# Splitting W_out's plain blocks in the projection's narrow groups instead of at the end of attention

## The chip, the cores and the metric

The kernel runs on one core of a Trainium2 chip. The metric is device time in microseconds of one execution, as the median over runs. A profile is of one execution, taken by the hardware profiler; its own time is given beside its span. The engines are PE (TensorE, matrix products), DVE (VectorE), ACT (ScalarE), POOL (GpSimd) and SP (SyncE, which here only issues DMAs).

## The reference

One decoder layer of width 1024 over 2048 tokens, in float32, followed by a last norm:

```python
n = rmsnorm(x)
# one projection W_in gives: GLA q, k, v, output gate and low-rank forget gate; attention q, k, v
a = gla_mixer(...)        # gated linear attention, 4 heads (dk 64, dv 128), chunks of 64
b = dilated_attention(...)  # 8 heads of 64; windows/dilations (128,1), (512,4), (2048,16), with a bias by distance
h = x + concat(a, b) @ W_out          # W_out is 1024 x 1024
h = h + relu(rmsnorm(h) @ W1) ** 2 @ W2   # 1024 -> 4096 -> 1024
y = rmsnorm_final(h)
```

The GLA half of the mix is normalised per head, and its gain `gn` is folded into the first 512 rows of W_out.

## The kernel before, in words

**Products in three passes.** A float32 factor is split into a part `hi`, rounded by ACT, and the rest `lo` = value − `hi`, by DVE. `mm3` (L139) issues hi·hi, lo·hi and hi·lo as three matmuls. So every matrix that PE uses is first split by ACT and DVE. The large products go through schemes with seven products for eight blocks, for which sums and differences of blocks are split.

**The projection** (up to about 490 us) runs over two halves of the tokens, in nine groups of columns of W_in for each half (NG = 9). Groups 2 to 7 are "narrow", 128 columns wide in each half of the columns, with seven products ("jobs") each, in the order 1, 2, 6, 5, 7, 3, 4. A job is twelve matmuls of 128x512. `prep` (L291) runs two jobs ahead of PE: ACT makes `hi` (L304), DVE makes `lo` (L306 or L308) and the sums of blocks of the weights, in place (L310, L313, L314, L316), into a ring of three buffers. SP loads the rows of W_in for the narrow groups, POOL those of the last, wide group (both L284, tile `wraw`); `finish` takes the results (L383, L384) and issues their stores (`qD`, `kD` and others). In the second half the narrow groups run from about 354 to 470 us, some 19 us each, and the last group, `gv`, from 470 to 490.

**Attention** (about 490 to 855 us) is written as 160 units, with GLA's steps, the loads of the next heads and the combination of the three branches (`mx`, L1439; its loads `combine_load`) issued between them at numbered units (`at_unit`, L1257; `plan`). PE's transposes there are L950, its products with v L969; ACT copies the probabilities (`pt`, L957) and evaluates the exponentials (L941), DVE makes the masked scores (L940) and some of the copies.

**W_out's product** follows (about 853 to 1032 us). Its matrix is taken as four column and row blocks. Some blocks are used as sums, made during attention by `sum_wo` and read by `mix_wo`; four, numbered 1, 12, 2 and 3, are used as they are ("plain"): by `product0` (L1605) for products 1, 2 and 3, and by `plain_rows` (L1619) for four tiles that take no scheme. `load_wo` (L1183) loads one of the eight 128-row pieces c of W_out (512 KB, tile `woraw`, L1188) at each of the units NU−28, NU−25, ..., and splits it at once: for c < 4 in two halves into the blocks 1 and 12 (ACT L1193 with the gain `gn`, DVE L1194), for c ≥ 4 in one piece into `wo` (ACT L543, DVE L544). That is between 788 and 847 us.

**Order and memory.** A scheduler with a cost model orders the instructions of each engine, unless `keep_in_program_order` holds one in its place; an engine then carries out its instructions strictly in that order, and waits for others by semaphores. All large tiles come from one pool of 25 slots of 128x2112 float32 (`slot`, L127); a slot's new tenant waits until the last reader of the old one is done. SP, ACT and POOL can issue DMAs, each in its own queue.

Of the kernel before, what the change touches and what calls it, by code (L numbers as in the profile page):

```python
# [10 lines left out]
F32 = mybir.dt.float32  # L11
FR = mybir.dt.float32r
I32 = mybir.dt.int32
AF = mybir.ActivationFunctionType
OP = mybir.AluOpType
# [3 lines left out]
D = 1024  # L19
NT = S // 128  # L20
HT = NT // 2
CH = D // 128
# [7 lines left out]
AHEAD, LAG = 3, 2  # L30
# [84 lines left out]
def emit(tc, a, stop=99):  # L115
    nc = tc.nc
    V, A, G, T, SP = nc.vector, nc.scalar, nc.gpsimd, nc.tensor, nc.sync
# [9 lines left out]
    def slot(name, dt=F32, n=SLOT):  # L127

        return up.tile([128, SLOT], dt, name=name, tag="u", bufs=25)[:, :n]

    def view(t, shape):
        n = int(np.prod(shape))
        names = "abcd"[:len(shape)]
        return t[:, :n].rearrange(f"p ({' '.join(names)}) -> p {' '.join(names)}", **dict(zip(names, shape)))
# [4 lines left out]
    def mm3(out, sh, sl, mh, ml, first, last, **kw):  # L139
        T.matmul(out, sh, mh, start=first, stop=False, **kw)  # L140
        T.matmul(out, sl, mh, start=False, stop=False, **kw)  # L141
        T.matmul(out, sh, ml, start=False, stop=last, **kw)  # L142
# [19 lines left out]
    gn = stats[:, 44:]  # L162
# [357 lines left out]
    def bias_rows():  # L520

        rb, oh, rbo = xp[:33, :8], view(xp[:33, 8:], (3, 384)), view(bp[:8], (3, 384))
        SP.dma_start(rb[:32], a["rel_bias"])
        SP.dma_start(oh, a["c_onehot"])
        V.memset(rb[32:33], NEG)
        yield
        V.tensor_scalar(rb[:32], rb[:32], -1.0, None, op0=OP.mult)
        for d in range(3):
            p = ps("d")
            T.matmul(p[:8, :384], rb, oh[:, d], start=True, stop=True)  # L530
            V.tensor_copy(rbo[:, d], p[:8, :384])
        SP.dma_start(rowD, rbo)
        yield
# [8 lines left out]
    def split(hi, lo, src):  # L542
        A.activation(hi, src, AF.Copy)  # L543
        V.tensor_tensor(lo, src, hi.bitcast(F32), op=OP.subtract)  # L544
# [60 lines left out]
    def second_half():  # L605

        b = [view(bp[:, 512 * q:], (4, 128)) for q in range(4)]
        for i in range(4):
            for k in range(2):
                x_load(8 + 4 * k + i, xp[:, D * k:D * k + D])  # L610
            yield
            for k in range(2):
                xt = xp[:, D * k:D * k + D]
                ss = stat()
                tc.keep_in_program_order(A.activation(bp[:, :D], xt, AF.Square, accum_out=ss))
                r = rstd_of(ss, D)
                V.scalar_tensor_tensor(xt, xt, r, gB, op0=OP.mult, op1=OP.mult)
            yield
            for k in range(2):
                for q, pv in enumerate(transposed(xp[:, D * k:], pin=True, by=perm)):  # L620
                    A.activation(b[2 * k + q], pv, AF.Copy)
                yield
            (b11, b21, b12, b22), (t2, t4, t3) = b, [view(xp[:, 512 * q:], (4, 128)) for q in range(3)]
            V.tensor_tensor(b12, b12, b11, op=OP.subtract)
            V.tensor_tensor(t2, b22, b12, op=OP.subtract)
            for j, v in ((2, b21), (1, b11), (5, b12), (6, t2), (3, b22), (4, t4), (7, t3)):
                if j == 5:
                    yield
                    V.tensor_tensor(t4, b21, t2, op=OP.subtract)
                    V.tensor_tensor(t3, t2, b11, op=OP.subtract)  # L630
                SP.dma_start(nTD[j - 1][:, :, i * 128:i * 128 + 128], v)
            yield
# [165 lines left out]
    SP.dma_start(w2b[33:50].bitcast(F32), w2raw[33:].bitcast(F32))  # L798
    for gT in gTs:
        A.activation(gT, ident, AF.Copy, scale=0.0)  # L800
    other, back, bias = second_half(), [], bias_rows()
    for at in range(7, len(jobs)):
        g = jobs[at][0]
        prep(at + 2)
        if at in (7 * NG - 7, 7 * NG - 6):
            back.extend(reload(2 * (at - 7 * NG + 7) + k) for k in range(2))
        for i in range(4 if groups[g % NG][2] > 128 else 1):
            ready = gated[:]
            product(at, i)()
            for t in ready:  # L810
                gate_product(t)
                gated.remove(t)
        if behind and chained(g):
            f, *args = behind.pop(0)
            f(*args)
        if back and at >= 7 * NG - 5:
            back.pop(0)()
            back.pop(0)()
        if at in OTHER:
            next(other)  # L820
        if at == len(jobs) - 14:
            heads = load_head(0)
        if at in (len(jobs) - 13, len(jobs) - 10, len(jobs) - 9):
            next(heads)
        if at in (7 * NG + 3, 7 * NG + 5):
            next(bias)
        if 7 * NG + 8 <= at < 7 * NG + 44 and at % 3 == 0:
            spread_bias(2 - (at - 7 * NG - 8) // 12, (at - 7 * NG - 8) // 3 % 4 * 2)
# [336 lines left out]
                    A.activation(st[:, j], st[:, j], AF.Copy, scale=w[:, j:j + 1])  # L1165
                yield

    wo = a["w_out"].rearrange("o (c p) n -> p (o c) n", p=128)
    WO, WB, loaded = {}, {}, []

    def block_view(j, c):

        if (j, c // 2) not in WB:
            WB[j, c // 2] = view(slot(f"wb{j}", FR), (2, 2, 512))
        return [WB[j, c // 2][:, c % 2, i] for i in range(2)]

    def wo_part(j, c):

        if j in (2, 3):
            return [WO[c][:, i, 512 * (j - 2):512 * (j - 2) + 512] for i in range(2)]  # L1180
        return block_view(j, c)

    def load_wo(n):  # L1183
        for _ in range(n):
            c = (4, 0, 1, 5, 2, 3, 6, 7)[len(loaded)]
            loaded.append(c)
            raw = slot("woraw")[:, :D]
            SP.dma_start(raw, wo[:, c])  # L1188
            if c < 4:
                for j, n in ((1, 0), (12, 1)):  # L1190
                    hi, lo = block_view(j, c)
                    r = raw[:, 512 * n:512 * n + 512]
                    A.activation(hi, r, AF.Copy, scale=gn[:, c:c + 1])  # L1193
                    V.scalar_tensor_tensor(lo, r, gn[:, c:c + 1], hi.bitcast(F32), op0=OP.mult, op1=OP.subtract)  # L1194
            else:
                w = WO[c - 4] = view(slot("wo", FR), (2, D))
                split(w[:, 0], w[:, 1], raw)

    wtD = dram.tile([4, 128, 2 * D], F32, name="wtD")

# [56 lines left out]
    def at_unit(n, *f):  # L1257
        plan.setdefault(n, []).append(f)
# [45 lines left out]
    NU = len(units)  # L1304
# [1 line left out]
    for n, x in enumerate(sums_wo):  # L1306
        at_unit(8 + AHEAD + n, next, x)
    for i in range(8):
        at_unit(NU - 28 + 3 * i + AHEAD, load_wo, 1)
    gla = gla_steps()  # L1310
    for k in range(-AHEAD, NU + LAG):
        tr, pv, sc = iter(()), iter(()), iter(())
# [292 lines left out]
    def product0(g):  # L1605
        p, j = g // 7, order[g % 7]
        if j in (1, 2, 5):
            held0[j] = ps({1: "a", 2: "o", 5: "d"}[j])
        b = held0[{6: 1, 7: 1, 4: 1, 3: 5}.get(j, j)]
        c = combs0[g % 6]  # L1610
        for k in range(4):
            mm3(b, c[:, 0, k], c[:, 1, k], *wo_part(j, k), k == 0 and j in (1, 2, 5), k == 3, skip_group_check=True)
        e, n = {1: (0, 0), 2: (0, 0), 6: (0, 1), 3: (0, 1), 5: (1, 1), 7: (1, 1), 4: (1, 0)}[j]
        x = xhs[p][:, e, 512 * n:512 * n + 512]
        V.tensor_tensor(x, b, x, op=OP.add)
        if j in (3, 4):
            row_done(p, j == 4)
# [9 lines left out]
    for at in range(4):  # L1627
        p, e = divmod(at, 2)
        m = nxt
        if at == 0:  # L1630
            load_x(0, True)
            tc.keep_in_program_order(SP.dma_start(gM, bcast_row(a["mlp_norm_g"], D)))
        if at in (0, 2):
            nxt = plain_rows(p, 1)
            load_mix(p + 1)
            load_x(p + 1)
        if at == 1:
            nxt = plain_rows(1, 0)
        mix_wo(at)
        if at == 3:  # L1640
            for n in range(4):
                raw_block(2, n % 2, n // 2)
            load_mix(3)
            for g in range(14, 16):
                prep0(g)
        b = [ps("ad"[e]), ps("ad"[e])]
        parts_ = 2 if at < 2 else 1
        for q in range(parts_):
            for n in range(2):
                for c in range(q * CH // parts_, (q + 1) * CH // parts_):  # L1650
                    mm3(b[n], m[:, 0, c], m[:, 1, c], *wo_part(((1, 12), (2, 3))[c // 4][n], c % 4), c == 0, c == CH - 1)
                if q == parts_ - 1:
                    x = xhs[p][:, e, 512 * n:512 * n + 512]
                    V.tensor_tensor(x, b[n], x, op=OP.add)
        next_norm()
        row_done(p, e)
        if at == 3:
            prep0(16)
# [270 lines left out]
```

## Time and profile before

| | |
|---|---|
| time, median of 3 runs | 2239.28 us (2235.93 to 2239.9) |
| profiled execution | 2235.3 us, span 2233.5 us, clock 0.998 |
| busy: PE, DVE, ACT, POOL | 99%, 74%, 55%, 24% of the span |
| narrow groups of the second half | about 354 to 470 us |
| attention | about 490 to 855 us |
| splits of W_out's plain blocks | 792.1 (first on ACT) to 845.5 us (last on DVE starts) |

A row of a timeline gives start and duration in us, the engine, the line of the kernel, the tile written and those read, the shape, and in brackets how long the engine stood idle before it and what ended that. A row of a window gives for each engine the busy time and, behind the x, the number of instructions, then the granted clock as a share of full speed, the busy share of the 16 DMA engines and what they moved in GB/s. A landing is the time from a DMA's issue to its arrival.

### The profile page before, as it was taken

The numbers are of one execution on the slowest core, as the hardware profiler recorded it, in microseconds if no ns is written. First come the engines' busy times: TensorE is split into PE (matmuls) and PEld (weight loads), VectorE is DVE, ScalarE is ACT, GpSimd is POOL, SyncE is SP. The second block draws the span as 40 slices with busy tenths as digits, with TensorE's granted clock in tenths as the row PEclk, the third lists the DMA queues.
The fourth block names the chain that finished last, engine by engine and source line by source line (L and its number), as shares of the span: only waits on it lengthen the run. The fifth ranks groups of instructions, "written<-read, shape, count | busy, mean of one in ns | idle before, by whom it ended". The sixth has DMA issues, their size and how long they took to land.

```text
span 2233.5 us, 34965 instructions
## 1 busy us (share of the span) xinstructions
PE 2208.3 (99%) x12420; PEld 1918.8 (86%) x12420; DVE 1650.9 (74%) x3093; ACT 1236.2 (55%) x2420; POOL 528.4 (24%) x527
## 2 busy tenths in 40 slices
PE   9999999999999999999999999999999999999998
PEld 8988998899999988887788887888888888888877
DVE  8676766657777788778776788777686697576798
ACT  7365524437888885546555566555555433333446
POOL 1000000026586673000000000000007222042462
PEclk9999999999999999999999999999999999999999
DMA  6566855677967966768644456555489998677775
GB/s 208 176 216 190 268 152 170 208 216 260 322 226 238 278 199 245 239 227 269 208 147 142 140 178 192 158 174 161 130 287 284 307 295 270 216 247 253 253 258 197
DMA packets 331763, 491.50 MB, mean 220 GB/s; under 512 B 20615, under 2 KB 225050, under 8 KB 320836
## 3 DMA queue, kind: packets, MB, share of 16 engines
q1 hardware_dynamic: 307282, 381.97, 52.7%
q0 software_dynamic: 16960, 54.60, 9.7%
q10 hardware_dynamic: 7346, 52.70, 6.2%
q8 instruction: 98, 1.61, 0.3%
q14 instruction: 77, 0.63, 0.1%
HBM read 335.25 MB, written 158.66 MB: 221 GB/s over the span
## 4 chain that ended last, share of the span: by engine, by line
PE 75%; issue 16%; DMA 3%; DVE 3%; POOL 2%; ACT 1%; POOLq 0%; ACTq 0%; SPq 0%; DVEq 0%
PE ps_a L141 8%; PE ps_a L142 8%; PE ps_a L140 8%; PE ps_c L141 6%; PE ps_c L142 6%; PE ps_c L140 6%; PE ps_a L969 4%; PE ps_d L141 4%; PE ps_d L142 4%; PE ps_d L140 4%; PE ps_o L140 3%; PE ps_o L141 3%; PE ps_o L142 3%; PE ps_d L950 3%; PE ps_c L932 2%
## 5 line engine op out<-in xcount | busy, mean ns | idle before, releaser
L543 ACT ACTIVATE cb<-bs 128x1024 fp32r<-128x1024 f32 x104 | 110.1, 1060 | 286.4 <-PE ps_c L141 95.4
L544 DVE TENSOR_TENSOR cb<-bs,cb 128x1024 fp32r<-128x1024 f32 x104 | 161.5, 1553 | 136.8 <-ACT cb L543 136.4
L1749 POOL TENSOR_TENSOR bs<-bs,rb 128x1024 f32<-128x1024 f32 x60 | 173.9, 2904 | 312.8 <-DMA bs<-w_ff 280.8
L544 DVE TENSOR_TENSOR w1comb<-w1raw,w1comb 128x512 fp32r<-128x512 f32 x224 | 153.5, 687 | 92.5 <-ACT w1comb L543 92.4
L1456 POOL DMA_DIRECT2D w1raw<-w_ff x64 | 48.1, 752 | 701.4 <-DVE w1comb L544 524.9
L543 ACT ACTIVATE w1comb<-w1raw 128x512 fp32r<-128x512 f32 x224 | 139.8, 627 | 89.1 <-PE ps_c L142 26.1
L969 PE MATMUL ps_a<-v,pt 128*128 128x65 f32 x1200 | 178.6, 253 | 1.8 <-ACT pt L957 1.8
L969 PEld LDWEIGHTS ps_a<-v,pt 128*128 128x128 f32 x1200 | 173.9, 195 | 3.8 <-ACT pt L957 2.7
L941 ACT ACTIVATE pe<-pe,O 128x256 f32<-128x256 f32 (+1 forms) x384 | 154.9, 453 | 13.5 <-DVE O L940 12.3
L950 PE MATMUL ps_d<-ident,pe 128*128 128x128 f32 x600 | 159.5, 280 | 1.2 <-ACT pt L957 1.1
L304 ACT ACTIVATE wcomb<-wraw 128x512 fp32r<-128x512 f32 (+2 forms) x119 | 90.4, 759 | 114.4 <-PE ps_a L141 54.6
L940 DVE CUSTOM_DVE_ANT_0 pe<-ps_c,nb 128x256 f32<-128x256 f32 (+1 forms) x384 | 125.7, 360 | 34.3 <-PE ps_d L950 23.0
L140 PE MATMUL ps_c<-hb,w1comb 128*128 128x512 f32 x320 | 124.6, 390 | 0.8 <-DVE acc L1545 0.8
L141 PE MATMUL ps_c<-hb,w1comb 128*128 128x512 f32 x320 | 124.5, 389 | 0.0
L142 PE MATMUL ps_c<-hb,w1comb 128*128 128x512 f32 x320 | 124.0, 389 | 0.0
L141 PE MATMUL ps_c<-cb,ca 128*128 128x512 f32 x312 | 121.4, 389 | 0.0
L142 PE MATMUL ps_c<-cb,ca 128*128 128x512 f32 x312 | 121.4, 389 | 0.0
L140 PE MATMUL ps_c<-cb,ca 128*128 128x512 f32 x312 | 121.4, 389 | 0.0
L544 DVE TENSOR_TENSOR ca<-ra,ca 128x1024 fp32r<-128x1024 f32 x84 | 119.7, 1426 | 0.1
L306 DVE TENSOR_TENSOR wcomb<-wraw,wcomb 128x512 fp32r<-128x512 f32 (+2 forms) x77 | 73.2, 950 | 53.3 <-ACT wcomb L304 53.2
L950 PEld LDWEIGHTS ps_d<-ident,pe 128*128 128x128 f32 x600 | 108.6, 186 | 1.7 <-ACT pt L957 1.3
L1530 ACT ACTIVATE acc<-acc 128x512 f32<-128x512 f32 x96 | 60.6, 632 | 68.3 <-DVE acc L1549 31.7
(490 smaller groups left out, 7174.4 us busy)
## 6 DMA issues: line engine op xcount, KB each, us to landing
ra<-actD ACTq DMA_DIRECT2D x50, 1024.0 KB, 7.4
actD<-ring SPq DMA_DIRECT2D x176, 256.0 KB, 3.0
rb<-w_ff SPq DMA_DIRECT2D x88, 512.0 KB, 5.9
bs<-w_ff SPq DMA_DIRECT2D x72, 512.0 KB, 6.6
w1raw<-w_ff POOLq DMA_DIRECT2D x64, 512.0 KB, 5.5
k<-kD SPq DMA_DIRECT2D x16, 1024.0 KB, 9.0
rb<-hTD SPq DMA_DIRECT2D x28, 512.0 KB, 5.0
wraw<-w_in SPq DMA_DIRECT2D x48, 256.0 KB, 3.7
```

The source lines that it names most:

```text
L140: T.matmul(out, sh, mh, start=first, stop=False, **kw)
L141: T.matmul(out, sl, mh, start=False, stop=False, **kw)
L142: T.matmul(out, sh, ml, start=False, stop=last, **kw)
L304: A.activation(hi, src, AF.Copy, scale=sc)
L306: V.tensor_tensor(lo, src, hi.bitcast(F32), op=OP.subtract)
L543: A.activation(hi, src, AF.Copy)
L544: V.tensor_tensor(lo, src, hi.bitcast(F32), op=OP.subtract)
L940: V.tensor_tensor_reduce(p, s, bias, scale=1.0, scalar=BIG, op0=OP.add, op1=OP.min, accum_out=nm)
L941: A.activation(p, p, AF.Exp, bias=nm, scale=-1.0)
L950: T.transpose(pb[:, i * 128:i * 128 + 128], src, ident)
L969: T.matmul(self.b.opsum[:, n % 4], self.pt[:, i * 128:i * 128 + 128], self.b.v[:, blk, cols], start=first, stop=last)
L1749: (engines or ((G,), (V, V))[len(sums) - 1])[e].tensor_tensor(v, v, r, op=OP.add if op == "+" else OP.subtract)
```

## The change

The eight 128-row pieces of W_out are loaded and split in the second half's narrow groups. A generator, `split_wo`, has two slots: one for two raw pieces of 512 KB (`wsum`), one for two split pieces (`wsplit`, each a half row of 512 columns as `hi` and `lo`). POOL loads the raw pieces; sixteen splits by ACT (L815 of the new file, held in program order) and DVE (L816) follow, two after each job 6 and two after each job 5 of groups 3 to 6 of the half; POOL stores each split piece (512 KB, L817) to DRAM, and after every second one loads the next raw piece (L819). At the end of attention, at the units at which `load_wo` ran, `load_parts` loads 1 MB of split pieces by SP (L1207) into the slots from which PE reads; neither ACT nor DVE takes part.

```diff
+    wsD = {j: dram.tile([2, 128, 2, 2, 512], F32, name=f"wsD{j}") for j in (1, 12, 2, 3)}
+    def split_wo():
+        raw, pieces = view(slot("wsum"), (2, D)), view(slot("wsplit", FR), (2, 2, 512))
+        for c in range(2):
+            G.dma_start(raw[:, c], wo[:, c])
+        yield
+        for n in range(16):
+            c, h = divmod(n, 2)
+            p = pieces[:, h]
+            r = raw[:, c % 2, 512 * h:512 * h + 512]
+            w = gn[:, c:c + 1] if c < 4 else 1.0
+            tc.keep_in_program_order(A.activation(p[:, 0], r, AF.Copy, scale=w))
+            V.scalar_tensor_tensor(p[:, 1], r, w, p[:, 0].bitcast(F32), op0=OP.mult, op1=OP.subtract)
+            G.dma_start(wsD[((1, 12), (2, 3))[c // 4][h]][c % 4 // 2, :, c % 2], p.bitcast(F32))
+            if h and c < 6:
+                G.dma_start(raw[:, c % 2], wo[:, c + 2])
+            yield
...
+        if at == 7 * NG + 18:
+            next(of_wo)
+        if NG + 3 <= g < NG + 7 and jobs[at][1] in (6, 5):
+            for _ in range(2):
+                next(of_wo)
...
-    def load_wo(n):
...
+    def load_parts(j, h):
+        t = slot(f"wb{j}", FR, 2048)
+        WB[j, h] = view(t, (2, 2, 512))
+        SP.dma_start(t.bitcast(F32), wsD[j][h].rearrange("p c i n -> p (c i n)"))
...
-        at_unit(NU - 28 + 3 * i + AHEAD, load_wo, 1)
+        at_unit(NU - 28 + 3 * i + AHEAD, load_parts, *((1, 0), (12, 0), (1, 1), (12, 1), (2, 0), (3, 0), (2, 1), (3, 1))[i])
...
-            mm3(b, c[:, 0, k], c[:, 1, k], *wo_part(j, k), k == 0 and j in (1, 2, 5), k == 3, skip_group_check=True)
+            mm3(b, c[:, 0, k], c[:, 1, k], *block_view(j, k), k == 0 and j in (1, 2, 5), k == 3, skip_group_check=True)
```

The order of ACT in a narrow group of the second half, before. `acc` are the results of the projection, `wcomb` the split weights of a job, `ps_a` and `ps_c` the accumulators:

```order
328 L304 ACTIVATE wcomb<-wraw 128x4x128 x2
329 L383 ACTIVATE acc<-acc 128x512
330 L482 ACTIVATE acc<-ps_a 128x4x16x8
331 L304 ACTIVATE wcomb<-wraw 128x4x128
332 L484 ACTIVATE acc<-ps_c 128x4x16x8
333 L304 ACTIVATE wcomb<-wraw 128x4x128 x2
334 L383 ACTIVATE acc<-acc 128x512
335 L304 ACTIVATE wcomb<-wraw 128x4x128
336 L383 ACTIVATE acc<-acc 128x512
```

The same place of ACT in the changed kernel:

```order
331 L304 ACTIVATE wcomb<-wraw 128x4x128 x2
332 L383 ACTIVATE acc<-acc 128x512
333 L482 ACTIVATE acc<-ps_a 128x4x16x8
334 L815 ACTIVATE wsplit<-wsum,stats 128x512 x2
335 L304 ACTIVATE wcomb<-wraw 128x4x128
336 L484 ACTIVATE acc<-ps_c 128x4x16x8
337 L304 ACTIVATE wcomb<-wraw 128x4x128 x2
338 L383 ACTIVATE acc<-acc 128x512
339 L304 ACTIVATE wcomb<-wraw 128x4x128
340 L815 ACTIVATE wsplit<-wsum,stats 128x512
341 L383 ACTIVATE acc<-acc 128x512
342 L815 ACTIVATE wsplit<-wsum,stats 128x512
```

Four splits of W_out now stand among a group's seven splits of W_in, two ahead of four L304 and two behind them.

The order of DVE around one change of groups, before. The L310 here reads the next group's rows of W_in:

```order
434 L306 TENSOR_TENSOR wcomb<-wraw,wcomb 128x4x128
435 L310 TENSOR_TENSOR wraw<-wraw 128x512
436 L384 TENSOR_TENSOR acc<-acc 128x512
437 L313 TENSOR_TENSOR wraw<-wraw 128x512
438 L492 TENSOR_TENSOR acc<-ps_c,acc 128x4x16x8
439 L306 TENSOR_TENSOR wcomb<-wraw,wcomb 128x4x128
440 L314 TENSOR_TENSOR wraw<-wraw 128x512
441 L384 TENSOR_TENSOR acc<-acc 128x512
```

And in the changed kernel:

```order
438 L306 TENSOR_TENSOR wcomb<-wraw,wcomb 128x4x128
439 L384 TENSOR_TENSOR acc<-acc 128x512
440 L313 TENSOR_TENSOR wraw<-wraw 128x512
441 L492 TENSOR_TENSOR acc<-ps_c,acc 128x4x16x8
442 L306 TENSOR_TENSOR wcomb<-wraw,wcomb 128x4x128
443 L816 SCALAR_TENSOR_TENSOR wsplit<-wsum,stats,wsplit 128x512
444 L314 TENSOR_TENSOR wraw<-wraw 128x512
445 L384 TENSOR_TENSOR acc<-acc 128x512
446 L310 TENSOR_TENSOR wraw<-wraw 128x512
447 L816 SCALAR_TENSOR_TENSOR wsplit<-wsum,stats,wsplit 128x512
```

L310 has moved from directly behind an L306 to behind seven more instructions, one of them a split of W_out; at the other changes of groups it moves by three to eight.

More of the change, by code (lines that the diff above doesn't have):

```diff
@@ L800, in emit @@
         A.activation(gT, ident, AF.Copy, scale=0.0)
+    wo = a["w_out"].rearrange("o (c p) n -> p (o c) n", p=128)
+    wsD = {j: dram.tile([2, 128, 2, 2, 512], F32, name=f"wsD{j}") for j in (1, 12, 2, 3)}
[15 more added lines that the diff above has]
+            yield
+    of_wo = split_wo()
     other, back, bias = second_half(), [], bias_rows()
@@ L1166, in gla_steps @@
                 yield
-    wo = a["w_out"].rearrange("o (c p) n -> p (o c) n", p=128)
-    WO, WB, loaded = {}, {}, []
+    WB = {}
     def block_view(j, c):
@@ L1175, in block_view @@
         return [WB[j, c // 2][:, c % 2, i] for i in range(2)]
[L1177 to L1181, printed above, removed]
-    def load_wo(n):
[L1184 to L1197, printed above, removed]
+    def load_parts(j, h):
+        t = slot(f"wb{j}", FR, 2048)
+        WB[j, h] = view(t, (2, 2, 512))
+        SP.dma_start(t.bitcast(F32), wsD[j][h].rearrange("p c i n -> p (c i n)"))
     wtD = dram.tile([4, 128, 2 * D], F32, name="wtD")
@@ L1650, in emit @@
                 for c in range(q * CH // parts_, (q + 1) * CH // parts_):
-                    mm3(b[n], m[:, 0, c], m[:, 1, c], *wo_part(((1, 12), (2, 3))[c // 4][n], c % 4), c == 0, c == CH - 1)
+                    mm3(b[n], m[:, 0, c], m[:, 1, c], *block_view(((1, 12), (2, 3))[c // 4][n], c % 4), c == 0, c == CH - 1)
                 if q == parts_ - 1:
```

## The prediction

> **What bounds the kernel now.** I read the page first (busy time, then the chain), then windows of 5 us over the end of attention, then PE's own timeline there with what ended each gap, then ACT's and DVE's timelines at those gaps, and last the narrow groups into which the work moves.
>
> ```profile
> PE 2208.3 (99%) x12420; PEld 1918.8 (86%) x12420; DVE 1650.9 (74%) x3093; ACT 1236.2 (55%) x2420; POOL 528.4 (24%) x527
> PE 75%; issue 16%; DMA 3%; DVE 3%; POOL 2%; ACT 1%; POOLq 0%; ACTq 0%; SPq 0%; DVEq 0%
> ```
>
> PE is busy for 99% of the span and carries three quarters of the chain. The change leaves PE's matmuls alone, so it can only give or take where PE stands still or runs slowly. The stage that loses its splitting work is such a place. Columns: PE busy (matmuls), PEld, DVE, ACT, POOL, granted clock, DMA share, GB/s.
>
> ```profile
> 800.00:805.00 5.00, 5.00 (x46) 4.82 (x46) 5.00 (x21) 4.43 (x13) 4.85 (x7) 1.00 0.34 132
> 805.00:810.00 5.00, 5.00 (x48) 4.60 (x47) 2.90 (x7) 3.52 (x13) 4.51 (x11) 1.00 0.90 266
> 810.00:815.00 5.00, 3.03 (x18) 2.09 (x17) 4.01 (x17) 2.93 (x6) 2.53 (x6) 0.90 0.93 316
> 815.00:820.00 5.00, 3.74 (x17) 3.74 (x18) 4.96 (x12) 3.39 (x10) 5.00 (x4) 0.50 0.62 215
> 820.00:825.00 5.00, 4.23 (x37) 4.03 (x35) 3.95 (x12) 4.28 (x10) 5.00 (x5) 0.91 0.28 104
> 825.00:830.00 5.00, 4.72 (x43) 4.72 (x44) 4.57 (x16) 5.00 (x14) 4.47 (x6) 1.00 0.74 225
> 830.00:835.00 5.00, 5.00 (x52) 5.00 (x51) 4.01 (x13) 4.80 (x15) 0.00 (x0) 1.00 1.07 314
> 835.00:840.00 5.00, 5.00 (x47) 4.89 (x46) 4.98 (x17) 4.71 (x17) 2.41 (x8) 1.00 0.99 295
> 840.00:845.00 5.00, 3.93 (x34) 3.54 (x33) 4.57 (x11) 4.40 (x9) 3.97 (x8) 1.00 0.73 232
> 845.00:850.00 5.00, 4.66 (x46) 4.68 (x47) 5.00 (x11) 4.94 (x14) 4.46 (x3) 1.00 1.00 329
> ```
>
> Undisturbed, PE does (46+48+52+47)/4 = 48.25 matmuls in 5 us. From 810 to 825 it does 18+17+37 = 72 where 144.75 were due: 72.75 missing, 7.5 us. From 825 to 830 and from 840 to 850 another 5.25+16.5 are missing, 2.3 us. So 9.8 us is lost here. PE's timeline names the gaps (start, duration, and in brackets the idle time before and what ended it):
>
> ```profile
> 812.43 1.13 PE L1160 MATMUL ps_o<-gla 128*128 128x256 f32 x4 [1.48 <-DVE gla L1107]
> 816.26 1.97 PE L969 MATMUL ps_a<-v,pt 128*128 128x65 f32 x8 [1.62 <-ACT pt L957]
> 825.28 0.66 PE L950 MATMUL ps_d<-ident,pe 128*128 128x128 f32 x4 [1.05 <-ACT pt L957]
> 845.34 0.53 PE L1439 MATMUL ps_c<-ident,mx 128*128 128x128 f32 x3 [1.41 <-DVE O L940]
> ```
>
> What stood ahead of the first, the second and the fourth:
>
> ```profile
> 810.23 1.34 ACT L1193 ACTIVATE wb<-woraw,stats 128x512 fp32r<-128x512 f32 x2 [1.71 <-DMA woraw<-w_out]
> 813.50 1.06 ACT L543 ACTIVATE wo<-woraw 128x1024 fp32r<-128x1024 f32 x1 [1.84 <-DMA woraw<-w_out]
> 842.04 2.00 DVE L544 TENSOR_TENSOR wo<-woraw,wo 128x1024 fp32r<-128x1024 f32 x1 [0.39 <-ACT wo L543]
> ```
>
> The first gap: ACT holds still 1.71 us for a raw row of W_out, DVE's L1194 waits for ACT's result, and the L1107 that PE needs is queued behind it. The second: ACT holds still 1.84 us for the next row, then splits it (1.06), and the `pt` copy L957 comes after. The fourth: 2.00 us of L544 stand on DVE ahead of the L940 that PE waits for. All four gaps together are 1.48+1.62+1.05+1.41 = 5.6 us; the other 4.2 of the 9.8 come mostly from the clock granted in 815–820, 0.50.
>
> **The change, part by part.** *Removed at the end of attention.*
>
> ```profile
> L1193 ACT ACTIVATE wb<-woraw,stats x8: 707/713/726, 801.3 to 830.5; 128x512 fp32r<-128x512 f32 x8
> L1194 DVE SCALAR_TENSOR_TENSOR wb<-woraw,stats,wb x8: 661/752/1743, 802.6 to 831.3; 128x512 fp32r<-128x512 f32 x8
> L543 ACT ACTIVATE wo<-woraw x4: 1043/1058/1058, 792.1 to 842.7; 128x1024 fp32r<-128x1024 f32 x4
> L544 DVE TENSOR_TENSOR wo<-woraw,wo x4: 1226/1656/2001, 793.2 to 845.5; 128x1024 fp32r<-128x1024 f32 x4
> DMA to landing us min/median/max: 3.6/3.8/4.1
> ```
>
> ACT loses 8×0.713 + 4×1.058 = 9.9 us, DVE 8×0.752 + 4×1.656 = 12.6 us, both from a stretch in which each is over 80% busy. More than the work, the waits go: nothing on ACT or DVE waits for `woraw` any more. All that is late next there is other attention work, which kept PE supplied in 800–810 and 830–840. The most that can come back is 9.8 us; the least is the idle of the two gaps whose ACT waited for a row, 1.48+1.62 = 3.1. I take the 7.5 us of 810–825 and leave the 2.3 us of the two later gaps to what follows.
>
> The Trainium skill ("TensorE: Matmul & The Clock Gate", Part 1: The HAM clock gate) has the clock halve only after an idle window of about 3.4 us. Here it stands at 0.50 after gaps of 1.48 and 1.62 us with work between them, so no single gap reaches the rule's length. By the rule alone the low clock would have another cause and stay, and the gain would be the idle only; the trace decides, since the low clock follows the two gaps and occurs in none of the other nine windows below 0.90.
>
> *Added at the end:* the eight loads are of 1 MB instead of 512 KB, 4.2 MB more on SP's queue, ahead of the `mx` and `gla` loads that attention itself waits for. The DMA shares of the ten windows leave 0.66+0.10+0.07+0.38+0.72+0.26+0.27 = 2.46 windows, 12.3 us, free; 4.2 MB at the 329 GB/s of the last row are 12.7. So they just fit, and a transfer behind one comes later.
>
> ```profile
> ra<-actD ACTq DMA_DIRECT2D x50, 1024.0 KB, 7.4
> ```
>
> The nearest row of that size lands in 7.4 us, 3.6 more than the 3.8 of a `woraw` row. The new loads themselves are issued by 838 and needed after 853, so their own 7.4 us lies hidden. For others behind them I take the 2.3 us already left out, between 0 and 3.6.
>
> *Added in the narrow groups:* sixteen ACT splits at the 0.713 of L1193, 11.4 us, sixteen on DVE at 0.752, 12.0 us, and 24 DMAs of 512 KB on POOL's queue, 12.6 MB. What stands there now, in windows of 10 us:
>
> ```profile
> 380.00:390.00 10.00, 10.00 (x47) 8.19 (x46) 5.58 (x11) 6.43 (x16) 0.00 (x0) 1.00 1.01 247
> 390.00:400.00 10.00, 10.00 (x46) 8.28 (x45) 8.02 (x13) 4.81 (x8) 0.00 (x0) 1.00 0.54 189
> 400.00:410.00 10.00, 10.00 (x46) 8.29 (x45) 4.60 (x7) 4.87 (x7) 0.00 (x0) 1.00 1.05 279
> 410.00:420.00 10.00, 9.73 (x43) 7.51 (x42) 7.43 (x11) 3.98 (x7) 0.00 (x0) 1.00 0.32 109
> 420.00:430.00 10.00, 10.00 (x46) 8.27 (x45) 4.81 (x8) 4.51 (x9) 0.00 (x0) 1.00 0.98 306
> 430.00:440.00 10.00, 10.00 (x46) 8.29 (x45) 8.27 (x13) 3.96 (x7) 0.00 (x0) 1.00 0.77 227
> 440.00:450.00 10.00, 10.00 (x46) 8.29 (x45) 4.50 (x7) 3.50 (x6) 1.51 (x2) 1.00 0.51 151
> 450.00:460.00 10.00, 10.00 (x46) 8.29 (x45) 4.44 (x7) 3.01 (x6) 0.00 (x0) 1.00 0.30 94
> sum 80.00, PE 79.73 PEld 65.41 DVE 47.65 ACT 35.07 POOL 1.51; mean PE 9.97 PEld 8.18 DVE 5.96 ACT 4.38 POOL 0.19
> ```
>
> In 80 us ACT has 45 us free and DVE 32, so 11.4 and 12.0 fit beside PE. Two waits are the danger. DVE's timeline shows the first, the transfers' rows the sizes (the last line is the landing of the 512 KB stores of `qD` in 355–470):
>
> ```profile
> 391.44 0.69 DVE L310 TENSOR_TENSOR wraw<-wraw 128x512 f32<-128x512 f32 x1 [1.88 <-DMA wraw<-w_in]
> 412.50 0.69 DVE L310 TENSOR_TENSOR wraw<-wraw 128x512 f32<-128x512 f32 x1 [3.46 <-DMA wraw<-w_in]
> 430.56 0.69 DVE L310 TENSOR_TENSOR wraw<-wraw 128x512 f32<-128x512 f32 x1 [2.03 <-DMA wraw<-w_in]
> wraw<-w_in SPq DMA_DIRECT2D x16, 256.0 KB, 5.6
> DMA to landing us min/median/max: 3.0/3.3/7.2
> ```
>
> First, DVE already stands 1.9 to 3.5 us at L310 in each of three groups, for the next group's rows of W_in; only the longest reached PE (43 matmuls for 46, 0.65 us). The new order puts L310 three to eight instructions of 0.69 us later, 2.1 to 5.5 us of relief, while POOL's transfers make those rows land later. Each group's rows, four loads of 256 KB, shared evenly with as many of POOL's bytes, come 1.05 MB/0.329 = 3.2 us later: about what the move gives. Of today's 3.46 us PE forgave 3.46−0.65 = 2.8, so the worst place would lose 3.46+3.2−2.1−2.8 = 1.8, the others nothing. Second, every split writes the piece that the store of two splits earlier reads, so ACT waits for that store; queued behind it are the splits L304 of W_in, for which DVE and then PE wait. Such a store lands in 3.3 us, 7.2 at worst. In ACT's new order four L304, one for each job of some 2.74 us (12 matmuls of 46 in 10 us), stand between a pair of splits and the pair that waits for it, so the store has landed. I take 1.3 for the first and 0.3 for each of four groups of splits, 2.5 us in all, between 0 and the 22 of the rival below. POOL has nothing else to do there (1.51 of 80 us busy); its loads of W_in for the last group come behind stores in its queue and are put at nothing as long as ACT's splits are in time; with those late, PE would stand at 470.
>
> *The sum:* 2235.3 − 7.5 + 2.5 = 2230.3 for the profiled execution. That one stood 4.0 below the median of the runs, 2239.28 (2235.93 to 2239.9), so the forecast for the median is **2234.3**, 5.0 or 0.22% less. A measurement here can tell about 0.2%, 4.5 us, from no change.
>
> **The rivals.** *Slower: POOL's transfers starve the rows of W_in.* In 380–390, 400–410 and 420–430 the DMA share is 1.01, 1.05 and 0.98 already, and the free shares of the eight windows are no more than 26 us, where 12.6 MB at 329 GB/s want 38. If a group's four stores and two loads (3.1 MB, 9.6 us) all go ahead of its rows of W_in, L310 waits 1.9+9.6, 3.5+9.6 and 2.0+9.6 us; less the 2.8 forgiven and the 2.1 to 5.5 of the move, that is 3.2 to 8.2 us on PE at each place, 11 to 22 in all. I price it at 12, near the low end, since a part of the transfers will come after the rows; that is also about where it decides, for less leaves it within 0.2%: 2235.3 − 7.5 + 12 = 2239.8, median 2243.8. With 22 it is 2253.8. For it: the shares. Against it: L310's later place, and PE's slack of two prepared jobs. The Trainium skill ("DMA: Bandwidth & Descriptors", Issuing engines are not separate DMA queues) says that transfers of every issuing engine interleave on the same sixteen engines; by that POOL's idle queue gives no room of its own, as the shares above 1 also have it.
>
> *No change: the gain is given back where it is made.* The 1 MB loads hold `mx` or `gla` up by 3.6 us once and the 0.50 clock comes back for part of a window: 2235.3 − 7.5 + 2.5 + 3.6 = 2233.9, median 2237.9. For it: the shares of 0.90 to 1.07 in six windows.
>
> *All of it:* 9.8 back and no cost ahead: 2225.5, median 2229.5. For it: the free time of ACT and DVE in the narrow groups; against it, the filled DMA engines.
>
> **How the numbers follow.** The forecast and the full gain hold 0.45 (0.31 and 0.14), no change 0.23, slower 0.32. The range leaves out half of the full gain's tail below 2227 and the worst of the starving above 2247, about 1 in 10 each. The forecast's own range, with 0 to 4.5 of costs and 7.5 to 9.8 of gain, is 2229.5 to 2236.5. Faster by over 0.2%: 0.45; within: 0.23; slower: 0.32.
>
> **What would show it.** Right: in the windows from 800 to 850 the matmul counts of 810–825 rise to about 48 each and the clock stays at 1.00; no ACT or DVE row waits for W_out. In the narrow groups PE loses under 4 us, and the new splits' idle before, put down to their own stores, stays small. Wrong: idle of DVE at L310 or of ACT at L815 of more than 4 us a group with gaps on PE behind it; a new wait for `mx` or `gla`; or the low clock in 815–820 without a gap.

## The result: slower by a quarter of a per cent

The changed kernel took 2243.28 us (median of 17 runs, 2239.02 to 2247.29) beside 2236.86 for the kernel before on the same chip (17 runs, 2232.8 to 2239.9). The ratio is 1.0025, with a 95% interval of 1.0016 to 1.0034: about 5.6 us more. A second measurement of the same file gave 1.0021 (1.0010 to 1.0032). The profiled execution took exactly the median. Its page begins:

```profile
span 2241.5 us, 35044 instructions
PE 2211.5 (99%) x12420; PEld 1919.0 (86%) x12420; DVE 1647.0 (73%) x3097; ACT 1239.8 (55%) x2424; POOL 537.3 (24%) x551
```

The end of attention did what was forecast. Windows there (columns as before):

```profile
805.00:810.00 5.00, 3.90 (x36) 3.68 (x36) 5.00 (x17) 2.78 (x8) 4.85 (x6) 1.00 0.27 85
810.00:815.00 5.00, 5.00 (x49) 5.00 (x48) 3.48 (x15) 4.72 (x18) 5.00 (x8) 1.00 0.97 371
815.00:820.00 5.00, 5.00 (x48) 4.90 (x47) 4.18 (x17) 4.97 (x14) 1.89 (x10) 1.00 1.00 320
820.00:825.00 5.00, 5.00 (x46) 4.89 (x46) 4.73 (x14) 4.12 (x11) 5.00 (x5) 1.00 1.07 422
```

From 810 to 825 PE does 143 matmuls where it did 72, at full clock. In 805–810 it does 36 where it did 48, behind a gap of 1.10 us at 807 that the kernel before does not have; the table below counts it. Lost instead is time in two other places. The first is the narrow groups:

```profile
410.00:420.00 10.00, 9.77 (x44) 7.75 (x42) 5.38 (x9) 4.16 (x7) 0.53 (x1) 1.00 1.07 346
420.00:430.00 10.00, 6.33 (x16) 4.77 (x17) 6.05 (x9) 3.38 (x8) 1.06 (x2) 0.66 1.03 334
430.00:440.00 10.00, 10.00 (x46) 8.25 (x45) 7.49 (x12) 5.13 (x9) 1.59 (x3) 1.00 1.04 335
```

Between 420 and 430 PE does 16 matmuls in place of 46. Its timeline, with those of ACT and DVE, and the landing times of the stores of the split pieces:

```profile
420.98 0.49 PE L140 MATMUL ps_a<-tb,wcomb 128*128 128x512 f32 x1 [1.21 <-ACT acc L482]
424.17 0.79 PE L141 MATMUL ps_a<-tb,wcomb 128*128 128x512 f32 x1 [2.69 <-DVE wcomb L306]
...
416.82 0.73 ACT L815 ACTIVATE wsplit<-wsum,stats 128x512 fp32r<-128x512 f32 x1 [4.49 <-DMA wsD<-wsplit]
...
417.58 0.75 DVE L816 SCALAR_TENSOR_TENSOR wsplit<-wsum,stats,wsplit 128x512 fp32r<-128x512 f32 x1 [4.03 <-ACT wsplit L815]
421.24 0.69 DVE L310 TENSOR_TENSOR wraw<-wraw 128x512 f32<-128x512 f32 x1 [1.71 <-DMA wraw<-w_in]
...
DMA to landing us min/median/max: 2.9/5.8/11.5
```

ACT holds still 4.49 us for the store of the split two before, DVE 4.03 us for ACT, and then DVE 1.71 us more for W_in's rows, so that L310 starts at 421.24 us where it started at 412.50 before. PE's first gap ends on ACT, which had stood for the store, the second on DVE, which had stood for ACT and then for the rows; the low clock is behind both.

The second place was not looked at in the forecast: the handover from W_out's product to the MLP (the two matrix products W1 and W2). First windows of before, then of after:

```profile
1030.00:1040.00 10.00, 8.50 (x41) 6.86 (x41) 9.24 (x13) 4.34 (x8) 1.50 (x2) 1.00 0.90 290
1040.00:1050.00 10.00, 10.00 (x46) 8.27 (x45) 9.26 (x13) 7.72 (x13) 0.00 (x0) 1.00 0.83 268
```

```profile
1030.00:1040.00 10.00, 6.24 (x32) 4.68 (x30) 7.62 (x10) 3.82 (x9) 1.50 (x2) 1.00 0.92 311
1040.00:1050.00 10.00, 10.00 (x37) 8.15 (x38) 8.80 (x14) 5.61 (x11) 0.00 (x0) 0.83 0.65 211
```

These are 69 matmuls for 87, about 3.9 us. PE and ACT in the timeline of before:

```profile
1038.04 0.50 PE L140 MATMUL ps_d<-hb,w1comb 128*128 128x512 f32 x1 [1.50 <-ACT w1comb L543]
...
1028.57 1.04 ACT L543 ACTIVATE hb<-rb 128x1024 fp32r<-128x1024 f32 x1
1029.61 1.04 ACT L543 ACTIVATE hb<-rb 128x1024 fp32r<-128x1024 f32 x1
1030.56 1.14 ACT L543 ACTIVATE w1comb<-w1raw 128x512 fp32r<-128x512 f32 x2
1037.36 0.63 ACT L543 ACTIVATE w1comb<-w1raw 128x512 fp32r<-128x512 f32 x1 [5.66 <-DMA w1raw<-w_ff]
```

And of after:

```profile
1032.84 0.50 PE L140 MATMUL ps_a<-hb,w1comb 128*128 128x512 f32 x1 [0.98 <-ACT w1comb L543]
1039.98 0.50 PE L140 MATMUL ps_d<-hb,w1comb 128*128 128x512 f32 x1 [2.78 <-ACT w1comb L543]
1059.38 0.73 PE L140 MATMUL ps_a<-hb,w1comb 128*128 128x512 f32 x2 [0.75 <-ACT w1comb L543]
...
1029.04 1.06 ACT L543 ACTIVATE hb<-rb 128x1024 fp32r<-128x1024 f32 x1 [0.89 <-DMA rb<-hTD]
1031.21 1.06 ACT L543 ACTIVATE hb<-rb 128x1024 fp32r<-128x1024 f32 x1 [0.16 <-DMA rb<-hTD]
1032.18 1.14 ACT L543 ACTIVATE w1comb<-w1raw 128x512 fp32r<-128x512 f32 x2
1039.30 0.63 ACT L543 ACTIVATE w1comb<-w1raw 128x512 fp32r<-128x512 f32 x1 [5.99 <-DMA w1raw<-w_ff]
```

In both kernels ACT splits four rows of the normed tokens (`hb`) before W1's first blocks (`w1comb`). But the order around them is another: two of these splits now stand ahead of the norm's sum of squares (`gs`) and not behind it. The other two wait for their rows here, 0.89 and 0.16 us, and PE waits 0.98 us for the blocks behind; before, ACT reached `w1comb` without such a wait, and PE had no gap at `ps_a`. The gap at `ps_d` is in both kernels, 1.50 us before and 2.78 after: ACT waits there for W1's next rows, 5.66 and 5.99 us.

To compare stages over many kernels, the table below gives PE's loss in each: the distance from each matmul's start to the next one's, less the median distance for the same line, tiles and shape in that kernel, summed over the stage. In attention ordinary waits are in the median, so sums there can be below zero; differences between kernels count. Each is of one execution, and executions of one kernel differ by 4 us either way; the ratios are of medians over 6 to 17 runs. They leave out two executions that took far longer, 2428.84 us of the kernel before and 6727.93 of wide_half.

| kernel | 380–490 | 800–860 | 1000–1120 | time to before (95%) |
|---|---|---|---|---|
| before | 0.8 | 6.5 | 5.6 | 1 |
| after | 7.9 | −1.4 | 10.7 | 1.0025 (1.0016–1.0034) |
| after_again | 7.3 | −0.4 | 11.0 | 1.0021 (1.0010–1.0032) |
| end_only | 0.4 | −2.2 | 10.7 | 0.9978 (0.9967–0.9989) |
| early_only | 6.8 | 4.5 | 5.8 | 1.0020 (1.0011–1.0030) |
| early_nostore | 4.0 | 6.2 | 7.3 | 1.0009 (0.9999–1.0020) |
| ring4 | 5.1 | 1.7 | 9.3 | 1.0006 (0.9996–1.0017) |
| ahead2 | 0.5 | 6.5 | 5.6 | 1.0006 (0.9993–1.0018) |
| half | 4.7 | 1.5 | 4.8 | 0.9998 (0.9986–1.0009) |
| end_spread | 0.1 | 1.0 | 11.7 | 1.0082 (1.0067–1.0098) |
| wide2 | 1.6 | −1.6 | 9.0 | 1.0007 (0.9995–1.0020) |
| wide_half | 0.0 | 0.8 | 5.5 | 0.9969 (0.9957–0.9981) |
| wide_24 | 1.8 | −0.7 | 10.8 | 0.9993 (0.9981–1.0004) |
| wide_wo | 0.3 | −0.3 | 4.0 | 0.9973 (0.9963–0.9984) |

For the changed kernel's profile: 7.1 us more in the narrow groups, 7.9 less at the end of attention, 5.1 more at the handover; by the same measure 1.9 more in 500–800, 1.8 more in W_out's product (860–1000) and 0.8 at the start. That is 8.8 for a span that is 8.0 longer.

### The profile page after: what moved, and what is told of

The parts are those of the page before. It is cut to its first block, busy times and chain, and to the rows that moved or that the text cites. A ratio compares the mean times of both kernels' runs of the same rounds, so it can differ in the third digit from the quotient of the medians.

```text
span 2241.5 us, 35044 instructions
## 1 busy us (share of the span) xinstructions
PE 2211.5 (99%) x12420; PEld 1919.0 (86%) x12420; DVE 1647.0 (73%) x3097; ACT 1239.8 (55%) x2424; POOL 537.3 (24%) x551
## 4 chain that ended last, share of the span: by engine, by line
PE 44%; issue 5%; DVE 2%; DMA 1%; POOL 0%; ACT 0%; POOLq 0%; DVEq 0%; ACTq 0%
PE ps_c L141 5%; PE ps_c L140 5%; PE ps_c L142 5%; PE ps_d L141 4%; PE ps_d L140 4%; PE ps_d L142 4%; PE ps_a L142 4%; PE ps_a L141 4%; PE ps_a L140 4%; PE ps_o L141 2%; PE ps_o L140 2%; PE ps_o L142 2%; DVE cb L544 0%; DMA w1raw<-w_ff 0%; DVE sum L1820 0%
## 5 line engine op out<-in xcount | busy, mean ns | idle before, releaser
L304 ACT ACTIVATE wcomb<-wraw 128x512 fp32r<-128x512 f32 (+2 forms) x119 | 90.3, 759 | 113.0 <-PE ps_a L141 54.3
L306 DVE TENSOR_TENSOR wcomb<-wraw,wcomb 128x512 fp32r<-128x512 f32 (+2 forms) x77 | 73.0, 948 | 49.4 <-ACT wcomb L304 49.4
L140 PE MATMUL ps_a<-wcomb,tb 128*128 128x256 f32 (+1 forms) x344 | 97.7, 284 | 0.0
```

The costliest lines, as they stand in the source:

```text
L304: A.activation(hi, src, AF.Copy, scale=sc)
```

## The experiments

**The two halves of the change, each alone.** end_only does nothing early, and its loads at the end read keys:

```diff
-        SP.dma_start(t.bitcast(F32), wsD[j][h].rearrange("p c i n -> p (c i n)"))
+        SP.dma_start(t.bitcast(F32), kD[{1: 0, 12: 1, 2: 2, 3: 3}[j]][:, h])
-        if at == 7 * NG + 18:
-            next(of_wo)
...
```

> Nothing is split or stored in the narrow groups; the eight loads of 1 MB at the end of attention read parts of attention's keys from DRAM in place of W_out's, so the values of the plain blocks are wrong and sizes, queue and places are those of the change. Its order in W_out's product and after it is word for word that of the changed kernel. Theory (the end of attention gains some 8 us, and the other order in W_out's product and at the handover to the MLP gives 6 back): 1 to 4 us less than before, PE's gaps at 800 to 850 gone, some 9 us lost in 1020 to 1080 against 3 before. Rival (the loss at the handover was of that one execution, or comes from the later start): 7 to 9 us less than before, and about 3 us lost at the handover.

Measured: 4.9 us less (0.9978), between the 1 to 4 of the theory and the 7 to 9 of the rival. Both its stages come out as the theory says: at 800–860 it gains 8.7, at the handover it loses 10.7 as the changed kernel does. PE there:

```profile
1026.09 0.50 PE L140 MATMUL ps_a<-hb,w1comb 128*128 128x512 f32 x1 [1.55 <-ACT w1comb L543]
1031.46 0.50 PE L140 MATMUL ps_d<-hb,w1comb 128*128 128x512 f32 x1 [1.01 <-ACT w1comb L543]
1049.27 0.73 PE L140 MATMUL ps_a<-hb,w1comb 128*128 128x512 f32 x2 [0.75 <-ACT w1comb L543]
```

Gaps at the same products as in the changed kernel, of other lengths, though the stage begins earlier and nothing was done in the narrow groups. The profiled run was the slowest of this kernel (2235.03, median 2230.75).

early_only keeps `split_wo` and takes the end from before:

```diff
-        at_unit(NU - 28 + 3 * i + AHEAD, load_parts, *(...)[i])
+        at_unit(NU - 28 + 3 * i + AHEAD, load_wo, 1)
```

> Splits and stores in the narrow groups as in the changed kernel, but the end of attention as before (raw rows loaded and split there; the stored parts are not read). Theory (the narrow groups cost what the profile shows there, 6 to 8 us): 6 to 8 us more than before, with a gap of PE of 3 to 4 us about 421 to 424 and the low clock behind it. Rival (the narrow groups cost little and the loss sits at the handover alone): within 2 us of before.

Measured: 4.5 us more (1.0020), less than the 6 to 8 of the theory, and outside the rival. The gap is there, in PE's timeline, and the handover is that of before (5.8):

```profile
418.99 0.51 PE L140 MATMUL ps_a<-tb,wcomb 128*128 128x512 f32 x1 [0.83 <-ACT acc L482]
422.69 0.50 PE L141 MATMUL ps_a<-tb,wcomb 128*128 128x512 f32 x1 [3.20 <-DVE wcomb L306]
```

In its profile 6.0 us more are lost in the narrow groups, and 2.0 less at the end of attention, which may be part of the difference.

**Which wait is it?** early_nostore leaves the stores out of early_only; ring4 gives the changed kernel a ring of four pieces:

```diff
-            G.dma_start(wsD[((1, 12), (2, 3))[c // 4][h]][c % 4 // 2, :, c % 2], p.bitcast(F32))
```

```diff
-            p = pieces[:, h]
+            if n == 2:
+                pieces.append(view(slot("wsplit", FR), (2, 2, 512)))
+            p = pieces[c % 2][:, h]
```

> As early_only, but the sixteen split pieces are not stored at all, so no split waits for a store and 8.4 MB less is moved; loads of the raw rows and all splits stay. Theory (ACT's wait for the store of two splits earlier is the cost): within 1.5 us of before, no wait of ACT at the splits over 1 us. Rival (the 23 us of splits themselves on ACT and DVE delay the preparation of W_in): 4 us or more above before.

> The changed kernel with four split pieces in the ring (a second slot) in place of two, so a split waits for the store of four splits earlier; as many stores and bytes. Theory (the wait for the store two back is the cost): 5 to 7 us less than the changed kernel, no gap of PE at 420 to 425. Rival (the DMA engines are full in these groups, and W_in's rows come late whatever the ring): within 2 us of the changed kernel, with the same 2 to 4 us gap of PE, now behind DVE's L310.

Measured: early_nostore 1.0009, ring4 1.0006, by the medians both better than the kernels from which they come (by 0.0015 to 0.0019 for ring4 and 0.0011 for early_nostore, where the intervals touch or overlap), neither free of the gap. No split waits for a store any more. The next lines are DVE and PE of early_nostore, then of ring4:

```profile
415.55 0.69 DVE L310 TENSOR_TENSOR wraw<-wraw 128x512 f32<-128x512 f32 x1 [5.44 <-DMA wraw<-w_in]
417.81 0.50 PE L141 MATMUL ps_c<-tb,wcomb 128*128 128x512 f32 x1 [3.13 <-DVE wcomb L306]
```

```profile
424.41 0.69 DVE L310 TENSOR_TENSOR wraw<-wraw 128x512 f32<-128x512 f32 x1 [6.06 <-DMA wraw<-w_in]
426.90 0.50 PE L140 MATMUL ps_a<-tb,wcomb 128*128 128x512 f32 x1 [2.27 <-ACT acc L482]
```

With the wait for the store gone, the wait of DVE at L310 for W_in's rows, 3.46 us before the change, has become 5.44 and 6.06, and PE stands still behind it. In the changed kernel it is 1.71, only because DVE comes to L310 later. So neither theory holds alone: the two waits hide one another. What they share is the third change of groups, where L310's wait was longest already.

The traces also show what holds the rows up. From the issue of the last of the group's four loads to L310's start it takes 5.6 us in the kernel before (406.91 to 412.50), 9.0 in early_nostore, where POOL issues two transfers of 512 KB between 404 and 410 us, 10.3 in half (below) and 12.8 in the changed kernel, both with three, and 15.1 in ring4, with six. The rows land the later, the more POOL has issued beside them.

**The dose.** half splits early only the pieces c < 4, two splits a group; the others are split at the end:

```diff
-        if NG + 3 <= g < NG + 7 and jobs[at][1] in (6, 5):
+        if NG + 3 <= g < NG + 7 and jobs[at][1] == 6:
...
-        for n in range(16):
+        for n in range(8):
```

> Only the pieces c < 4 (blocks 1 and 12) are split in the narrow groups, two splits a group after job 6, so 4 raw loads and 8 stores instead of 8 and 16; the pieces c >= 4 are loaded and split at the end of attention as before. Theory (the narrow cost comes from the bytes, whether ACT waits for a store or DVE for W_in's rows): PE loses under 3 us in 380 to 490 against 7 to 8 in the changed kernel, no wait for a store, and the time is 0 to 4 us less than before. Rival (any early split delays the third change of groups): the gap of some 3 us at 415 to 425 stays, and the time is 2 us or more above before.

Measured: 0.9998, between the two. PE and DVE:

```profile
418.83 0.80 PE L141 MATMUL ps_c<-tb,wcomb 128*128 128x512 f32 x1 [2.87 <-DVE wcomb L306]
...
417.48 0.69 DVE L310 TENSOR_TENSOR wraw<-wraw 128x512 f32<-128x512 f32 x1 [5.84 <-DMA wraw<-w_in]
```

The gap at the third change stays with half the bytes (4.7 us lost in the stage, against the expected "under 3"), as the rival says; the time, 0.4 us less, is at the edge of the theory's 0 to 4. It is no test of the bytes at this place: at the third change POOL issues three transfers in half as in the changed kernel, and what is saved comes later. At 800–860 half takes back 5.0 of the 6.5 us with two thirds of ACT's splits gone, so the work, or the waits, of the pieces c < 4 are the larger part there.

**Waits or work at the end?** ahead2 was to take ACT's waits for raw rows away and leave the work:

```diff
+        at_unit(NU - 28 + 3 * i + AHEAD, fetch_wo, 1)
-        at_unit(NU - 28 + 3 * i + AHEAD, load_wo, 1)
+        at_unit(NU - 28 + 3 * i + 2 + AHEAD, load_wo, 1)
```

> The kernel before, with each raw row of W_out loaded at the same unit as before and split two units (about 4.6 us) later; nothing is done in the narrow groups, and ACT and DVE do all the splits at the end of attention. Theory A (ACT's waits for the rows, 1.71 and 1.84 us, make the first two gaps and the low clock): 4 to 7 us less than before, no wait of ACT for the rows, the clock at 1.00 in 810 to 825. Theory B (it is the 23 us of splitting on ACT and DVE itself): within 2 us of before, gaps of over 1 us on PE remain in 800 to 850.

It does not tell: the first line is the work of the splits, the second the idle time of their engines.

```profile
L1199 ACT ACTIVATE wb<-woraw,stats x8: 707/709/723, 801.8 to 829.7; 128x512 fp32r<-128x512 f32 x8
  DMA woraw<-w_out: 5.6, 5
```

The splits still start from 801.8 to 829.7 (801.3 to 830.5 before): the scheduler's order left them where they were, and ACT and DVE still stand 5.6 us for the rows. The time, 1.0006, is that of before. Whether the waits alone would have been worth removing stays open.

**Once more, and the handover.** after_again is the changed kernel itself; end_spread is end_only with `NU - 40 + 4 * i` in place of `NU - 28 + 3 * i`.

> The changed kernel once more, for a second profile and to be compared with its parts on one chip. Theory (the costs in the narrow groups and from W_out's product on lie in its order and its transfers, and recur): 4 to 7 us above before; in the profile PE loses 5 to 8 us in 380 to 490 with the gap at 418 to 425, and 9 to 12 us in 1000 to 1120 against some 6 in kernels with the old order. Rival (end_only and early_only add, and the first measurement and profile were a bad draw): within 2 us of before, with other gaps.

> As end_only (no early work, the eight loads read parts of the keys in place of W_out's parts, wrong values), but the loads are issued from 40 units before the end on, one in four units instead of one in three; the order of W_out's product and of what follows comes out different from both kernels'. Theory (the loss in W_out's product and at the handover belongs to the order that the scheduler makes there): PE's gaps in 900 to 1120 are others than the set that end_only, ring4 and the changed kernel share (0.98 to 1.55 at ps_a, then 1.0 to 2.8 at ps_d, 0.75, 0.3, 0.52, 0.9), and the time is 3 to 10 us less than before. Rival (the loss comes from the loads being of 1 MB and landing late, or from the time at which the stage begins): the same set of gaps, the time 4 to 6 us less than before.

after_again repeats all three stages (table) and the time. So the changed kernel is slower indeed, though end_only and early_only, 4.9 less and 4.5 more, add up to nothing and not to 5; the parts' intervals, some 2 us either way each, do not close that. end_spread lost 18 us (1.0082) where both theories had a gain. Its PE:

```profile
794.30 2.07 PE L1107 MATMUL ps_o<-gla 128*128 128x256 f32 x4 [2.82 <-POOL gla L1097]
1042.94 0.80 PE L140 MATMUL ps_a<-hb,w1comb 128*128 128x512 f32 x1 [2.94 <-ACT w1comb L543]
```

The loads come into GLA's last steps, where new gaps appear; why was not followed up. For the handover it is no test of the order: W_out's product came out in another order, but the handover itself (ACT's word for word) in that of the changed kernel, and 11.7 us are lost there.

wide2 moves the sixteen splits to the wide group, wide_24 also the loads at the end (24 for 28), wide_half moves half's eight:

```diff
-        if at == 7 * NG + 18:
+        if at == 7 * NG + 2:
             next(of_wo)
-        if NG + 3 <= g < NG + 7 and jobs[at][1] in (6, 5):
+        if 7 * NG + 4 <= at < 7 * NG + 12:
```

> The changed kernel with its sixteen splits and stores moved from the narrow groups 3 to 6 to jobs 4 to 11 of the second half (beside the wide group gr, about 290 to 375 us, where ACT is busy 11% to 48% and the DMA engines 21% to 63% in the profile of before); the order at the end of attention, in W_out's product and after it is that of the changed kernel. Theory (the narrow groups' 7 us come from full DMA engines there, the rest of the loss from the order after attention): 5 to 8 us less than the changed kernel, that is 0 to 4 less than before; PE loses under 2 us in 240 to 490 beside before's, and the handover's set of gaps stays, 9 to 12 us in 1000 to 1120. Rival (16 splits and 12.6 MB cost some 5 us wherever they stand): no more than 2 us less than the changed kernel.

> wide2 with the eight loads of 1 MB issued from 24 units before the end on in place of 28, at which the order of W_out's product and of what follows comes out different from the changed kernel's (nearer to that of before, but not the same). Theory (the loss of 6 us from W_out's product on belongs to that order): a set of gaps in 900 to 1120 other than that of the changed kernel. If it is the loads' size or landing: the same set, 0.98 to 1.55 at ps_a, 1.0 to 2.8 at ps_d, 0.75, 0.3 to 0.8, 0.52, 0.9. Time 0 to 8 us less than before by the first, 0 to 4 by the second.

> half (only the pieces c < 4 split early, the others at the end as before) with its eight splits moved to jobs 4 to 11 of the second half; its order after attention is that of half, near that of before. Theory: without the 4 us that half loses in 415 to 430, and with a handover of some 5 us lost in 1000 to 1120, it is 3 to 7 us less than before, the fastest correct kernel so far. Rival (the gain of half at the end of attention is given back in 500 to 800): within 2 us of before.

All three lose under 2 us in 380–490, which the splits have left. Where they stand now, in 240–380, PE loses 0.6 us more than before in wide2, 2.0 in wide_24 (and 3.8 in wide_wo, below) and nothing in wide_half, against 7.1 in the narrow groups. The DMA share in 320–340 is 1.01 in wide2 too; why the same work costs less there is not shown. wide2, 1.0007 against 1.0025 and 1.0021, gains about 3 to 4 us on the changed kernel, less than the 5 to 8 expected, and loses 9.0 at the handover; wide_24 loses 10.8; its expectation took the order there to be a new one, but the trace has the changed kernel's, so the run does not tell the order from the loads. wide_half, whose handover has the order of before, loses 5.5 there and takes 0.9969 (0.9957 to 0.9981): 6.9 us less than before. By then every kernel with the old order at the handover lost 4.8 to 7.3 in 1000–1120, and every one with the new order 9.0 to 11.7. The seven kernels with the new order all have a gap of 0.98 to 2.94 us at the first `ps_a` of the MLP and one of 0.74 or 0.75 some 23 to 27 us later, and no kernel with the old order has either; the gap at `ps_d` is in both kinds (2.48 in half, none over 0.3 in wide2). But all of the second kind also had eight loads of 1 MB and no block left to split at the end.

wide_wo parts these. It is wide2 with the parts of c ≥ 4 kept by row in DRAM and in the slots, as before has them:

```diff
+            to = wsD[(1, 12)[h]][c // 2, :, c % 2] if c < 4 else woD[c - 4][:, :, 512 * h:512 * h + 512]
+            G.dma_start(to, p.bitcast(F32))
```

> wide2 with the parts of the pieces c >= 4 kept by row (one slot of 1024 columns hi and lo for each piece, as the kernel before has them) in place of by block; the sixteen early splits, the bytes and the eight loads of 1 MB at the same units stay. With that the scheduler puts the handover to the MLP (ACT word for word, PE all but) in the order of before; W_out's product itself comes out in a further order. Theory (the handover's 4.7 us belong to the order there): PE loses 5 to 7 us in 1000 to 1120 against 9 to 12 in the kernels with the changed order, and the time is 4 to 7 us less than wide2, that is 3 to 6 less than before. Rival (they come from eight loads of 1 MB, or from all blocks being split early): 9 us or more lost in 1000 to 1120, and the time within 2 us of wide2.

Measured: 0.9973 (0.9963 to 0.9984), 6 us less than before and some 7 to 8 less than wide2. The handover loses 4.0, below the 5 to 7 expected. ACT and PE there:

```profile
1022.76 2.01 ACT L543 ACTIVATE hb<-rb 128x1024 fp32r<-128x1024 f32 x2 [0.50 <-PE ps_d L142]
1027.38 1.13 ACT L543 ACTIVATE w1comb<-w1raw 128x512 fp32r<-128x512 f32 x2
1034.70 0.50 PE L140 MATMUL ps_d<-hb,w1comb 128*128 128x512 f32 x1 [1.34 <-ACT w1comb L543]
```

`w1comb` no longer stands behind a wait for `rb`, the first gap is gone and the second is 1.34. The loads' size, their number and the early splits are as in wide2, so the handover's cost goes with the order there, and the order with how the blocks of c ≥ 4 lie in their slots. (The order of the loads is another too in wide_wo; half, which loads the blocks 1 and 12 first as the changed kernel does, has the old order at the handover as well.) Why the scheduler orders by that is not known. This kernel still loses 3.8 us more than before in 340–380, where the moved splits now stand: the two best kernels are not the end of it.

## Why the prediction was wrong

- *End of attention:* right, 7.5 forecast, 7.9 and 6.9 measured by PE's loss, with the clock at 1.00. The low clock went with the gaps, as read there. The rule quoted from the Trainium skill ("TensorE: Matmul & The Clock Gate", Part 1: The HAM clock gate) would have left it, and it came again at 420–430 behind gaps of 1.21 and 2.69 us, each under its 3.4: here the measurement decides against a single idle window of that length.
- *"For others behind them":* PE stands for `mx` behind the 1 MB loads, 0.78 us in the changed kernel and 1.82 in after_again, within the 0 to 3.6. That the loads cause it is not shown: early_only, without them, has 1.12.
- *Narrow groups:* the term of 2.5 was mis-sized; it measured 7.1 and 6.5. Two steps failed. One is "so the store has landed". Four L304 did stand between the two pairs of splits, but ACT ran them from 405.62 to 411.70, in 6 us and not in four jobs' 11, and the store issued at 406.20 landed only some 10 us later, not in the 3.3 to 7.2 taken from a stage with less traffic. The bound "7.2 at worst" was no bound once 12.6 MB were added to it. The other is that W_in's rows would come 3.2 us later, "about what the move gives": at the third change they took 12.8 us from issue to use where they took 5.6, 7.2 us more.
- *The rival of the starved rows* had the cause right (DMA shares of 1.03 to 1.07 in 410–440) and the wait only in part: L310 waits 1.71 us in the changed kernel, and 6.06 as soon as ACT waits less. Its price of 12 was too high and its "decides from 12" counted nothing else. That its median, 2243.8, is almost the one measured is luck: the narrow groups cost 7.1, and the rest came from a stage that it did not look at.
- *Missing:* the step that decided the sign. "The change leaves PE's matmuls alone, so it can only give or take where PE stands still" was taken to mean the two stages of the diff. The order of the engines at the handover, some 170 us after attention, had changed too, PE's own included; it was there to be read, and was read only for the two stages. It costs about 5 us at the handover and, less surely, 2 us in W_out's product. With 7.1 for 2.5 and 5 for nothing, the sum −5.0 becomes +4.6, against 5.6 by the ratio of the medians.

## What to carry to other kernels

Where a scheduler orders the instructions, compare the whole order, not that of the stages that the diff names: here a different layout of four buffers went with another order in a later stage, which cost two thirds of what the change could bring. A transfer's landing time holds only at the traffic at which it was read; with a stage's DMA share near 1, ask for the landing with the new bytes added. And two waits behind one cause hide each other: remove one, look at the other, and then try the work at another place.

## What the runs showed of the hardware

Stores of 512 KB from POOL landed in 2.9 to 11.5 us in one stage, by the traffic beside them, and rows loaded by SP in the same stage (256 KB each) could be used 5.6 us after the issue with none of POOL's transfers beside them and 15.1 us after it with six (before and ring4). A clock below full (0.50, 0.66 and 0.83 in the windows shown) came behind gaps of 1.0 to 2.8 us. The length of a gap alone does not say whether it comes: wide2 has a clock of 0.64 in 1028–1032 behind a single gap of 1.90 us, the kernel half has 1.00 throughout 1040–1055 behind one of 2.48. What decides is not known from these runs. And executions of one program on one core spread over 8 us (2239.02 to 2247.29), more than this change is worth, so that single profiles place a loss but do not size it.
